# State space branch of a two-block model on one core: states of four pairs kept, output products issued by column group, input products on full-height tiles

## Chip, cores and metric

One Trainium2 chip, one core. The metric is the device time of one execution in microseconds (us). Three runs of the kernel before gave 3057.99, 3059.45 and 3059.55 us; the median is 3059.45 us.

## The reference

The kernel computes two blocks of a network on 256 tokens of width 2048 (272 tokens with 16 meta tokens in the first block). Block one projects the normed input into query and key-value latents, a signal u of width 1024 and two gates, runs latent attention and a diagonal state space model side by side, mixes both, and applies a feed-forward layer. Block two has an mLSTM layer and a banded attention layer. Only the state space model is touched by the change:

```
bu  = einsum(u, B_bar)                    # per group of 16 channels, 64 complex states
x_t = A_bar * x_{t-1} + bu_t              # 272 steps, complex
y   = Re(C x) + D u
y   = gelu(y);  ssm_out = (y @ w_val) * sigmoid(y @ w_gate)
```

There are 64 channel groups. Two of them make a *pair* (128 states, 32 channels), so there are 32 pairs, and they lie in eight blocks j of four pairs q.

## The kernel before, in words

**The main stream.** Nearly all work of TensorE is weight products in a two-part form. `split_chunk` (L397 to L406) loads a chunk of eight 128x128 weight blocks on SyncE's queue, ScalarE casts it to `hi` (L404), VectorE forms `lo = raw - hi` (L405); there are five `raw`, three `hi` and three `lo` buffers. `mm3` then issues for each block one product with `hi` over 512 columns (L430) and one with `lo` over 256 columns (L434); L432 and L433 take the place of L430 where 272 tokens are worked on. `Stream.take` counts a *tick* whenever a new chunk is begun, and each tick advances the side tasks that have been spawned.

**The side task.** `ssm` is a generator; `run` spawns it as `self.paced(self.ssm(), 2)`, so that one of its steps (from `yield` to `yield`) is written into the program every second tick, while the main stream works on the latents, the gates, attention (`mla`) and its projection (`attn_proj`). Before `ssm_out` and `mix` the task is finished. The order in which each engine then gets its instructions is set by a planner that simulates the program (`schedule_with_timeline_sim=True`); writes into one PSUM tile keep the order of the program.

**One turn of `ssm`** (g = 0 to 3) works on two blocks j = 2g and 2g+1, that is on eight pairs, and treats pair q of both blocks (index k = 0, 1) together:
- `ssm_matrices(j)` (L882 to L934): a 384 KB load issued from ScalarE's queue (L887) into the first 768 columns of `ssa[:, k, :]`, VectorE products of [128, 128] (L898 to L903, L919, L920 and others), four transposes (L909) into columns 768 to 1279, output matrices in columns 1280 to 1791, scratch `t1`, `t2` in columns 1792 to 2047, and the products for `k0` (L928). Those loop over q outside and the two parts i inside; each writes 32 partitions of PSUM, a column group of the array of its own for each q.
- 16 copies of u into `uu` (L958), in the form of [64 rows per pair]: two pairs share one tile, in its upper and lower half.
- for each q: four **input products** (L972), with a stationary tile of 64 rows and 128 columns over 136 columns; the rotation tables `cs`, `sn` (L975 to L980); a step later the rotated inputs (L982 to L987) and the scans (L992, L993); a step later the states `xr`, `xi` (L997 to L1002); a step later ten **output products** (L1009 to L1013), five for each k. Four of the five have 128 rows and 32 columns (L1009, L1010, L1012, L1013); the one with `k0` (L1011) has 32 rows and 32 columns. All ten of a pair write the same 32 partitions of the PSUM tile `yps`, which is taken at the head of the turn.
- at the end two additions into `yv` (L1017).

The states lie in `ws[2]` and `ws[4]`, which the tables of the next q overwrite (L976 writes `ws[2]`). Every fp32 product shows in the trace as two instructions ("x2"), each with its own weight load.

Of the kernel before, what the change touches and what calls it, by code (L numbers as in the profile page):

```python
# [8 lines left out]
F32 = mybir.dt.float32  # L9
# [3 lines left out]
ALU = mybir.AluOpType  # L13
AX = mybir.AxisListType

P = 128
D = 2048
KT = D // P
T = 256
NM = 16  # L20
TM = T + NM
# [279 lines left out]
class Builder:  # L301
# [50 lines left out]
    def sm(self, n=32):  # L352
        return self.t("s", [P, 32], bufs=20)[:, :n]
# [399 lines left out]
    def ssm_setup(self):  # L753
        nc = self.nc
        V = nc.vector
        w = self.pair(1, TM, dtype=F32).rearrange("p i k t -> p i (k t)")

        self.ssa, self.ssw = w[:, 0, :4096].rearrange("p (k n) -> p k n", k=2), w[:, 1, :]
        sm = self.sm
        ts = lambda o, x, s1, s2, op0, op1: V.tensor_scalar(o, x, s1, s2, op0, op1)  # L760
        tt = V.tensor_tensor
# [48 lines left out]
        step, x, mag = sm(), sm(), sm()  # L810
# [12 lines left out]
        nr, den, a, b = (sm() for _ in range(4))  # L823
# [17 lines left out]
        w = self.ssw  # L841
# [94 lines left out]
    def ssm(self):  # L936
        nc = self.nc
        yield from self.ssm_setup()
        tt = nc.vector.tensor_tensor
        mm = nc.tensor.matmul  # L940
        scan = nc.vector.tensor_tensor_scan
        NCH = TM // 2
        ws = [self.ssw[:, 1600 + i * TM : 1600 + (i + 1) * TM] for i in range(8)]
        cs, sn = ws[0], ws[1]

        uu = self.ssw[:, 1600 + 8 * TM : 1600 + 10 * TM].rearrange("p (k h c) -> p k h c", k=2, h=2)
        two = lambda ap: ap.rearrange("p (k c) -> p k c", k=2)
        m = lambda ap: ap.rearrange("p (k a b) -> p k a b", k=2, a=17)

        for g in range(4):  # L950
            k0 = []
            for j in (2 * g, 2 * g + 1):
                k0.append((yield from self.ssm_matrices(j)))
            for k in range(2):
                for q in range(4):
                    for e in range(2):
                        r = 64 * (q % 2) + 32 * e
                        nc.vector.tensor_copy(  # L958
                            uu[r : r + 32, k, q // 2, :], self.u[32 * q : 32 * q + 32, 2 * g + k, e, :]
                        )  # L960
            yield
            yps = self.aux()
            for q in range(4):
                rows = slice(32 * q, 32 * q + 32)
                p0 = slice(8 * g + q, 8 * g + q + 5, 4)
                pr, pi = self.aux(TM), self.aux(TM)
                r2 = slice(64 * (q % 2), 64 * (q % 2) + 64)
                for k in range(2):
                    c = slice(k * NCH, (k + 1) * NCH)
                    for ps, i in ((pr, 0), (pi, 1)):  # L970
                        o = 768 + 256 * i + P * (q // 2)
                        mm(ps[:, c], self.ssa[r2, k, o : o + P], uu[r2, k, q // 2, :], start=True, stop=True)  # L972
                a_ = [x[:, p0, :].unsqueeze(3).to_broadcast([P, 2, 17, 8]) for x in self.tabA]
                b_ = [x[:, p0, :].unsqueeze(2).to_broadcast([P, 2, 17, 8]) for x in self.tabB]
                tt(m(cs), a_[0], b_[0], ALU.mult)  # L975
                tt(m(ws[2]), a_[1], b_[1], ALU.mult)  # L976
                tt(cs, cs, ws[2], ALU.subtract)
                tt(m(sn), a_[1], b_[0], ALU.mult)
                tt(m(ws[3]), a_[0], b_[1], ALU.mult)
                tt(sn, sn, ws[3], ALU.add)  # L980
                yield
                tt(ws[2], pr, cs, ALU.mult)  # L982
                tt(ws[3], pi, sn, ALU.mult)
                tt(ws[2], ws[2], ws[3], ALU.add)
                tt(ws[4], pi, cs, ALU.mult)
                tt(ws[5], pr, sn, ALU.mult)
                tt(ws[4], ws[4], ws[5], ALU.subtract)  # L987
                for k in range(2):
                    c = slice(k * NCH, (k + 1) * NCH)
                    i = 8 * g + 4 * k + q  # L990
                    d = self.mag2[:, i : i + 1].to_broadcast([P, NCH])
                    scan(ws[3][:, c], d, ws[2][:, c], 0.0, ALU.mult, ALU.add)  # L992
                    scan(ws[5][:, c], d, ws[4][:, c], 0.0, ALU.mult, ALU.add)  # L993
                yield

                x = lambda ap: two(ap)[:, :, NM // 2 - 1 :]
                tt(x(ws[2]), x(ws[3]), x(cs), ALU.mult)  # L997
                tt(x(ws[6]), x(ws[5]), x(sn), ALU.mult)
                tt(x(ws[2]), x(ws[2]), x(ws[6]), ALU.subtract)
                tt(x(ws[4]), x(ws[5]), x(cs), ALU.mult)  # L1000
                tt(x(ws[7]), x(ws[3]), x(sn), ALU.mult)
                tt(x(ws[4]), x(ws[4]), x(ws[7]), ALU.add)  # L1002
                yield
                for k in range(2):
                    w = self.ssa[:, k, :]
                    o = k * NCH + NM // 2
                    xr, xi = ws[2][:, o - 1 :], ws[4][:, o - 1 :]
                    ev, od = yps[rows, k * T : k * T + P], yps[rows, k * T + P : (k + 1) * T]
                    mm(ev, w[:, 1536:1664][:, rows], xr[:, :P], start=True, stop=False)  # L1009
                    mm(ev, w[:, 1664:1792][:, rows], xi[:, :P], start=False, stop=False)  # L1010
                    mm(ev, k0[k][rows, :], self.u[rows, 2 * g + k, 0, NM // 2 :], start=False, stop=True)  # L1011
                    mm(od, w[:, 1280:1408][:, rows], xr[:, 1 : P + 1], start=True, stop=False)  # L1012
                    mm(od, w[:, 1408:1536][:, rows], xi[:, 1 : P + 1], start=False, stop=True)  # L1013
            eo = lambda ap: ap.rearrange("p (c e) -> p e c", e=2)
            for k in range(2):
                j = 2 * g + k
                nc.vector.scalar_tensor_tensor(  # L1017
                    eo(self.yv[:, j, :]), self.u[:, j, :, NM // 2 :], self.v("ssm_d", j),
                    two(yps[:, k * T : (k + 1) * T]), ALU.mult, ALU.add,
                )  # L1020
# [577 lines left out]
    def run(self):  # L1598
        self.setup()
        self.front()  # L1600
        self.ssm_in()
        ssm = self.spawn(self.paced(self.ssm(), 2))
        self.latents()
        self.conditioning(((150, 476), (510, 770)))
        self.gates()
        heads = self.mla()
        self.attn_proj(heads)
        self.finish(ssm)
        self.ssm_out()
        self.mix()  # L1610
        self.out_proj()
        self.ffn()
        self.enter2()
        self.probe("x1", self.x)
        state = self.layer0()
        while self.later:
            self.later.pop(0)[1]()
        self.layer1(*state)
# [33 lines left out]
```

## Time and profile before

| what | value |
|---|---|
| median of 3 runs | 3059.45 us |
| the profiled execution | 3057.36 us |
| span of its trace | 3055.6 us |
| busy: PE, VectorE, ScalarE, GpSimd | 98%, 76%, 48%, 2% |
| mean granted TensorE clock | 0.989 |
| chain that ended last | PE 97%, VectorE 2%, ScalarE 1% |
| the state space branch in the trace | about 47 to 600 us, from 128 us on with products |

The profiled execution is one run of its own. Its span is counted from the first to the last instruction; 1.8 us lie around it. A matmul's row gives its start and a modelled duration that overlaps the next one's, so the cost of a product is read from the distance between starts.

### The profile page before, as it was taken

The numbers are of one execution on the slowest core, as the hardware profiler recorded it, in microseconds if no ns is written. First come the engines' busy times: TensorE is split into PE (matmuls) and PEld (weight loads), VectorE is DVE, ScalarE is ACT, GpSimd is POOL, SyncE is SP. The second block draws the span as 40 slices with busy tenths as digits, with TensorE's granted clock in tenths as the row PEclk, the third lists the DMA queues.
The fourth block names the chain that finished last, engine by engine and source line by source line (L and its number), as shares of the span: only waits on it lengthen the run. The fifth ranks groups of instructions, "written<-read, shape, count | busy, mean of one in ns | idle before, by whom it ended". The sixth has DMA issues, their size and how long they took to land.

```text
span 3055.6 us, 46404 instructions
## 1 busy us (share of the span) xinstructions
PE 2998.4 (98%) x17170; PEld 2573.7 (84%) x17170; DVE 2327.8 (76%) x4641; ACT 1479.0 (48%) x2360; POOL 75.4 (2%) x139
## 2 busy tenths in 40 slices
PE   8899999999999999999999999999999999999987
PEld 8878888788888888888888888888888888888876
DVE  7988855689888778878878878877777778546555
ACT  5433355455544444434455444444444555445554
POOL 0000000000000000000000000000000001000000
PEclk9999999999999999999999999999999999999998
DMA  7545522498878888878756677778777765665544
GB/s 243 164 144 174 173 83 83 146 318 273 275 274 277 270 279 270 278 267 268 262 182 200 227 259 249 249 261 268 257 256 250 236 188 183 188 193 179 178 158 129
DMA packets 187139, 673.06 MB, mean 220 GB/s; under 512 B 21280, under 2 KB 23456, under 8 KB 186656
## 3 DMA queue, kind: packets, MB, share of 16 engines
q1 hardware_dynamic: 179568, 649.12, 65.3%
q0 software_dynamic: 4128, 15.73, 1.5%
q10 hardware_dynamic: 3216, 5.24, 0.5%
q8 instruction: 134, 2.20, 0.3%
q14 instruction: 93, 0.76, 0.1%
HBM read 661.63 MB, written 8.39 MB: 219 GB/s over the span
## 4 chain that ended last, share of the span: by engine, by line
PE 97%; DVE 2%; ACT 1%; issue 0%; POOL 0%; DMA 0%; SPq 0%; ACTq 0%; DVEq 0%; POOLq 0%
PE acc L430 50%; PE acc L434 26%; PE acc L479 3%; PE acc L478 3%; PE acc L477 3%; PE acc L432 1%; PE acc L433 1%; PE aux L972 1%; PE aux L1071 1%; PE aux L1383 0%; DVE lo L405 0%; PE aux L1070 0%; PE aux L1540 0%; PE aux L1361 0%; PE aux L1012 0%; PE aux L1011 0%
## 5 line engine op out<-in xcount | busy, mean ns | idle before, releaser
L430 PE MATMUL acc<-big,hi 128*128 128x512 f32 x6592 | 2323.6, 397 | 8.3 <-DVE big L1220 3.0
L434 PE MATMUL acc<-big,lo 128*128 128x256 f32 (+1 forms) x6832 | 1912.9, 282 | 2.2 <-DVE lo L405 2.0
L404 ACT ACTIVATE hi<-raw 128x1024 fp32r<-128x1024 f32 (+1 forms) x969 | 1025.5, 1059 | 1304.4 <-PE acc L430 807.1
L405 DVE TENSOR_TENSOR lo<-raw,hi 128x1024 fp32r<-128x1024 f32 (+1 forms) x969 | 1183.1, 1221 | 558.2 <-ACT hi L404 550.9
L430 PEld LDWEIGHTS acc<-big,hi 128*128 128x128 f32 x6592 | 1237.8, 188 | 297.7 <-issue 5.3
L434 PEld LDWEIGHTS acc<-big,lo 128*128 128x128 f32 x6832 | 1288.8, 189 | 14.6 <-DVE lo L405 4.2
L626 DVE SCALAR_TENSOR_TENSOR raw<-raw,gemv 128x512 f32<-128x512 f32 x512 | 332.2, 685 | 0.0
L477 PE MATMUL acc<-hi,big 128*128 128x512 f32 (+1 forms) x480 | 178.0, 371 | 0.3 <-DVE qr L442 0.3
L478 PE MATMUL acc<-hi,big 128*128 128x512 f32 (+1 forms) x480 | 177.3, 369 | 0.0
L479 PE MATMUL acc<-lo,big 128*128 128x512 f32 (+1 forms) x480 | 169.2, 375 | 0.0
L442 DVE TENSOR_TENSOR t<-t,acc 128x256 f32<-128x256 f32 x276 | 114.0, 414 | 6.7 <-ACT t L441 6.6
L441 ACT ACTIVATE t<-acc 128x256 f32<-128x256 f32 x276 | 100.9, 367 | 14.0 <-PE acc L434 12.1
L477 PEld LDWEIGHTS acc<-hi,big 128*128 128x128 f32 x480 | 90.1, 188 | 16.0 <-DVE qr L442 0.6
L478 PEld LDWEIGHTS acc<-hi,big 128*128 128x128 f32 x480 | 90.2, 188 | 15.3 <-issue 0.3
L479 PEld LDWEIGHTS acc<-lo,big 128*128 128x128 f32 x480 | 89.4, 188 | 15.5 <-issue 1.0
L432 PE MATMUL acc<-big,hi 128*128 128x272 f32 x240 | 70.2, 295 | 7.9 <-ACT hi L404 7.9
L447 DVE TENSOR_TENSOR big<-big,acc 128x256 f32<-128x256 f32 x160 | 65.3, 415 | 13.2 <-PE acc L434 12.4
L433 PE MATMUL acc<-big,hi 128*128 128x272 f32 x240 | 69.9, 293 | 0.0
L489 DVE TENSOR_TENSOR ss<-ss,t 128x256 f32<-128x256 f32 (+1 forms) x132 | 54.5, 422 | 2.5 <-ACT t L488 2.1
L432 PEld LDWEIGHTS acc<-big,hi 128*128 128x128 f32 x240 | 46.0, 192 | 8.8 <-ACT hi L404 7.9
L1323 DVE SCALAR_TENSOR_TENSOR t<-qr,vec,t 128x256 f32<-128x256 f32 x96 | 46.1, 480 | 1.0
L433 PEld LDWEIGHTS acc<-big,hi 128*128 128x128 f32 x240 | 46.1, 192 | 0.0
(360 smaller groups left out, 1953.2 us busy)
## 6 DMA issues: line engine op xcount, KB each, us to landing
raw<-in_w_l_dram SPq DMA_DIRECT2D x482, 512.0 KB, 4.2
raw<-in_w_ffn_dram SPq DMA_DIRECT2D x264, 512.0 KB, 4.4
raw<-in_w_ada_dram SPq DMA_DIRECT2D x256, 512.0 KB, 4.5
raw<-in_w_in_dram SPq DMA_DIRECT2D x97, 512.0 KB, 3.7
raw<-in_w_mix_dram SPq DMA_DIRECT2D x64, 512.0 KB, 4.4
raw<-in_w_out_dram SPq DMA_DIRECT2D x32, 512.0 KB, 4.5
raw<-in_w_up_dram SPq DMA_DIRECT2D x28, 512.0 KB, 3.5
gates_d<-qa POOLq DMA_DIRECT2D x16, 256.0 KB, 2.9
```

Of the source, the lines that this page charges most:

```text
L404: nc.scalar.activation(hi[:, c], raw[:, c], AF.Copy)
L405: self.last_lo = nc.vector.tensor_tensor(lo[:, c], raw[:, c], hi[:, c].bitcast(F32), ALU.subtract)
L430: mm(both, wh, x[:, :, kt, :], start=(kt == 0), stop=False)
L432: mm(ps[:, :n], wh, x[:, 0, kt, :], start=(kt == 0), stop=False)
L433: mm(ps[:, :n], wh, x[:, 1, kt, :], start=False, stop=False)
L434: mm(ps[:, :n], wl, x[:, 0, kt, :], start=False, stop=last)
L441: self.nc.scalar.activation(dst, ps[:, n : 2 * n], AF.Copy)
L442: self.nc.vector.tensor_tensor(dst, dst, ps[:, :n], ALU.add)
L477: mm(ps, xh[:, kt, b:e], wh, start=(kt == 0), stop=False)
L478: mm(ps, xl[:, kt, b:e], wh, start=False, stop=False)
L479: mm(ps, xh[:, kt, b:e], wl, start=False, stop=(kt == nk - 1))
L626: nc.vector.scalar_tensor_tensor(raw[:, j, :], raw[:, j, :], 0.5, st["c"], ALU.mult, ALU.mult, accum_out=st["sum"][:, 2 * i + j : 2 * i + ...
```

## The change

The states of all four pairs of a turn get buffers of their own (`xs`): five of the eight in the columns 0 to 644 of `ssa`, which hold the loaded matrices until they have been used, one in the scratch columns from 1792 on, two in `ssw`. The ten output products of the four pairs leave the loop over q and come after one more `yield`, the loop over q innermost, so that four products in a row write the four column groups. `yps` is taken only then. `uu` has a tile of 128 rows for each q and k, zero outside the pair's 64 rows, zeroed once on GpSimd; the input products take all 128 rows. The copies take both k at once: 8 in place of 16 for a turn. `ws` has five buffers in place of eight. A further `yield` stands ahead of the additions into `yv`.

```diff
-        w = self.pair(1, TM, dtype=F32).rearrange("p i k t -> p i (k t)")
-        self.ssa, self.ssw = w[:, 0, :4096].rearrange("p (k n) -> p k n", k=2), w[:, 1, :]
+        w = self.pair(1, TM, dtype=F32).rearrange("p i k t -> p (i k t)")
+        self.ssa, self.ssw = w[:, :4096].rearrange("p (k n) -> p k n", k=2), w[:, 4096:]
...
+        uu = self.ssw[:, o : o + 8 * NCH].rearrange("p (k q c) -> p k q c", k=2, q=4)
+        nc.gpsimd.memset(uu, 0.0)
+        xs = [self.ssa[:, :, i * NX : (i + 1) * NX] for i in range(5)] + [self.ssa[:, :, 1792 : 1792 + NX]]
...
-                        mm(ps[:, c], self.ssa[r2, k, o : o + P], uu[r2, k, q // 2, :], start=True, stop=True)
+                        mm(ps[:, c], self.ssa[:, k, o : o + P], uu[:, k, q, :], start=True, stop=True)
...
-                for k in range(2):
-                    w = self.ssa[:, k, :]
...
-                    mm(ev, w[:, 1536:1664][:, rows], xr[:, :P], start=True, stop=False)
-                    mm(ev, w[:, 1664:1792][:, rows], xi[:, :P], start=False, stop=False)
-                    mm(ev, k0[k][rows, :], self.u[rows, 2 * g + k, 0, NM // 2 :], start=False, stop=True)
-                    mm(od, w[:, 1280:1408][:, rows], xr[:, 1 : P + 1], start=True, stop=False)
-                    mm(od, w[:, 1408:1536][:, rows], xi[:, 1 : P + 1], start=False, stop=True)
+
+            yps = self.aux()
+            for k in range(2):
+                w = self.ssa[:, k, :]
+                for o, n, i, c0 in ((0, 1536, 0, 0), (0, 1664, 1, 0), (0, None, 0, 0), (P, 1280, 0, 1), (P, 1408, 1, 1)):
+                    for q in range(4):
+                        rows = slice(32 * q, 32 * q + 32)
+                        out = yps[rows, k * T + o : k * T + o + P]
+                        if n is None:
+                            mm(out, k0[k][rows, :], self.u[rows, 2 * g + k, 0, NM // 2 :], start=False, stop=True)
+                        else:
+                            mm(
+                                out, w[:, n : n + P][:, rows], xs[2 * q + i][:, k, c0 : c0 + P],
+                                start=(i == 0), stop=(c0 == 1 and i == 1),
+                            )
+            yield
```

## Rows read from the trace of the kernel before

**Rows 1.** The page: shares of the chain that ended last.
```profile
PE 97%; DVE 2%; ACT 1%; issue 0%; POOL 0%; DMA 0%; SPq 0%; ACTq 0%; DVEq 0%; POOLq 0%
```

**Rows 2.** Busy time by stretch: length, PE, PEld, DVE, ACT, POOL, clock, DMA share, GB/s.
```profile
160.00:380.00 220.00, 220.00 (x1341) 178.85 (x1339) 190.44 (x451) 77.36 (x106) 10.37 (x15) 1.00 0.54 167
380.00:600.00 220.00, 219.49 (x1373) 174.32 (x1373) 133.18 (x317) 109.97 (x259) 6.13 (x13) 1.00 0.33 102
```

**Rows 3.** Timeline of PE, one pair's output products: start, duration, instruction, count.
```profile
206.29 0.40 PE L430 MATMUL acc<-big,hi 128*128 128x512 f32 x1
206.52 0.28 PE L434 MATMUL acc<-big,lo 128*128 128x256 f32 x1
206.65 0.39 PE L430 MATMUL acc<-big,hi 128*128 128x512 f32 x1
...
212.93 0.39 PE L430 MATMUL acc<-big,hi 128*128 128x512 f32 x1
213.25 0.41 PE L1009 MATMUL aux<-big 128*32 128x128 f32 x2
213.59 0.39 PE L434 MATMUL acc<-big,lo 128*128 128x256 f32 x1
...
214.25 0.41 PE L1010 MATMUL aux<-big 128*32 128x128 f32 x2
...
215.16 0.38 PE L1013 MATMUL aux<-big 128*32 128x128 f32 x2
215.38 0.38 PE L1009 MATMUL aux<-big 128*32 128x128 f32 x2
...
216.80 0.50 PE L430 MATMUL acc<-big,hi 128*128 128x512 f32 x1
217.13 0.28 PE L434 MATMUL acc<-big,lo 128*128 128x256 f32 x1
```

**Rows 4.** Timeline of PE: the small products L928, alone and in a burst.
```profile
220.85 0.25 PE L928 MATMUL aux<-big 128*32 128x32 f32 x2
221.03 0.66 PE L909 MATMUL aux<-cst,big 128*128 128x128 f32 x4
...
227.91 0.48 PE L928 MATMUL aux<-big 128*32 128x32 f32 x28
228.33 0.39 PE L434 MATMUL acc<-big,lo 128*128 128x256 f32 x1
```

**Rows 5.** Timeline of PE: input products, and full-height fp32 products (L909).
```profile
162.79 0.28 PE L434 MATMUL acc<-big,lo 128*128 128x256 f32 x1
163.00 0.73 PE L972 MATMUL aux<-big 64*128 64x136 f32 x4
163.66 0.50 PE L430 MATMUL acc<-big,hi 128*128 128x512 f32 x1
...
187.80 0.38 PE L909 MATMUL aux<-cst,big 128*128 128x128 f32 x2
187.93 0.36 PE L434 MATMUL acc<-big,lo 128*128 128x256 f32 x1
188.13 0.40 PE L430 MATMUL acc<-big,hi 128*128 128x512 f32 x1
```

**Rows 6.** Line L972: count, min/median/max ns, first and last start.
```profile
L972 PE MATMUL aux<-big x128: 276/276/592, 128.7 to 562.7; 64*128 64x136 f32 x128
```

**Rows 7.** Waits of DVE, 128 to 620 us: total, times, longest.
```profile
DVE big L976 <- PE aux L1012: 17.5, 8, 3.2
```

**Rows 8.** DMA issues, one line: count, KB each, us to landing.
```profile
big<-in_ssm_dram ACTq DMA_DIRECT2D x8, 384.0 KB, 4.4
```

**Rows 9.** Lines L900, L1017, L1131: count, min/median/max ns, first and last start.
```profile
L900 DVE TENSOR_TENSOR big<-big x16: 277/284/293, 76.6 to 439.4; 128x128 f32<-128x128 f32 x16
L1017 DVE SCALAR_TENSOR_TENSOR big<-big,vec,aux x8: 473/479/483, 216.9 to 598.7; 128x256 f32<-128x256 f32 x8
L1131 DVE SCALAR_TENSOR_TENSOR big<-t,t x16: 399/418/426, 568.8 to 648.3; 128x256 f32<-128x256 f32 x16
```

More of the change, by code (lines that the diff above doesn't have):

```diff
@@ L942, in ssm @@
         NCH = TM // 2
-        ws = [self.ssw[:, 1600 + i * TM : 1600 + (i + 1) * TM] for i in range(8)]
-        cs, sn = ws[0], ws[1]
-        uu = self.ssw[:, 1600 + 8 * TM : 1600 + 10 * TM].rearrange("p (k h c) -> p k h c", k=2, h=2)
+        NX = T // 2 + 1
+        ws = [self.ssw[:, 1600 + i * TM : 1600 + (i + 1) * TM] for i in range(5)]
+        cs, sn, t1, t2, t3 = ws
+        o = 1600 + 5 * TM
+        uu = self.ssw[:, o : o + 8 * NCH].rearrange("p (k q c) -> p k q c", k=2, q=4)
+        nc.gpsimd.memset(uu, 0.0)
+        xs = [self.ssa[:, :, i * NX : (i + 1) * NX] for i in range(5)] + [self.ssa[:, :, 1792 : 1792 + NX]]
+        rest = self.ssw[:, o + 8 * NCH : o + 8 * NCH + 4 * NX].rearrange("p (k i c) -> p k i c", k=2, i=2)
+        xs += [rest[:, :, 0, :], rest[:, :, 1, :]]
         two = lambda ap: ap.rearrange("p (k c) -> p k c", k=2)
@@ L953, in ssm @@
                 k0.append((yield from self.ssm_matrices(j)))
-            for k in range(2):
[L955 to L960, printed above, removed]
+            for q in range(4):
+                for e in range(2):
+                    r = 64 * (q % 2) + 32 * e
+                    nc.vector.tensor_copy(
+                        uu[r : r + 32, :, q, :], self.u[32 * q : 32 * q + 32, 2 * g : 2 * g + 2, e, :]
+                    )
             yield
-            yps = self.aux()
             for q in range(4):
-                rows = slice(32 * q, 32 * q + 32)
                 p0 = slice(8 * g + q, 8 * g + q + 5, 4)
                 pr, pi = self.aux(TM), self.aux(TM)
-                r2 = slice(64 * (q % 2), 64 * (q % 2) + 64)
                 for k in range(2):
@@ L975, in ssm @@
                 tt(m(cs), a_[0], b_[0], ALU.mult)
-                tt(m(ws[2]), a_[1], b_[1], ALU.mult)
-                tt(cs, cs, ws[2], ALU.subtract)
+                tt(m(t1), a_[1], b_[1], ALU.mult)
+                tt(cs, cs, t1, ALU.subtract)
                 tt(m(sn), a_[1], b_[0], ALU.mult)
-                tt(m(ws[3]), a_[0], b_[1], ALU.mult)
-                tt(sn, sn, ws[3], ALU.add)
+                tt(m(t2), a_[0], b_[1], ALU.mult)
+                tt(sn, sn, t2, ALU.add)
                 yield
-                tt(ws[2], pr, cs, ALU.mult)
@@ L983, in ssm @@
[L983 to L993, printed above, removed]
+                tt(t1, pr, cs, ALU.mult)
@@ new lines, in ssm @@
+                tt(t2, pi, sn, ALU.mult)
+                tt(t1, t1, t2, ALU.add)
+                tt(t2, pi, cs, ALU.mult)
+                tt(t3, pr, sn, ALU.mult)
+                tt(t2, t2, t3, ALU.subtract)
+                for a, b in ((t1, t3), (t2, t1)):
+                    for k in range(2):
+                        c = slice(k * NCH, (k + 1) * NCH)
+                        i = 8 * g + 4 * k + q
+                        scan(b[:, c], self.mag2[:, i : i + 1].to_broadcast([P, NCH]), a[:, c], 0.0, ALU.mult, ALU.add)
@@ L994, in ssm @@
                 yield
                 x = lambda ap: two(ap)[:, :, NM // 2 - 1 :]
[L997 to L1002, printed above, removed]
-                yield
-                for k in range(2):
-                    w = self.ssa[:, k, :]
-                    o = k * NCH + NM // 2
-                    xr, xi = ws[2][:, o - 1 :], ws[4][:, o - 1 :]
-                    ev, od = yps[rows, k * T : k * T + P], yps[rows, k * T + P : (k + 1) * T]
-                    mm(ev, w[:, 1536:1664][:, rows], xr[:, :P], start=True, stop=False)
-                    mm(ev, w[:, 1664:1792][:, rows], xi[:, :P], start=False, stop=False)
-                    mm(ev, k0[k][rows, :], self.u[rows, 2 * g + k, 0, NM // 2 :], start=False, stop=True)
-                    mm(od, w[:, 1280:1408][:, rows], xr[:, 1 : P + 1], start=True, stop=False)
-                    mm(od, w[:, 1408:1536][:, rows], xi[:, 1 : P + 1], start=False, stop=True)
@@ new lines, in ssm @@
+                xr, xi = xs[2 * q], xs[2 * q + 1]
+                tt(xr, x(t3), x(cs), ALU.mult)
+                tt(x(t2), x(t1), x(sn), ALU.mult)
+                tt(xr, xr, x(t2), ALU.subtract)
+                tt(xi, x(t1), x(cs), ALU.mult)
+                tt(x(t2), x(t3), x(sn), ALU.mult)
+                tt(xi, xi, x(t2), ALU.add)
+                yield
+            yps = self.aux()
+            for k in range(2):
+                w = self.ssa[:, k, :]
+                for o, n, i, c0 in ((0, 1536, 0, 0), (0, 1664, 1, 0), (0, None, 0, 0), (P, 1280, 0, 1), (P, 1408, 1, 1)):
+                    for q in range(4):
+                        rows = slice(32 * q, 32 * q + 32)
[6 more added lines that the diff above has]
+                                start=(i == 0), stop=(c0 == 1 and i == 1),
+                            )
```

## The prediction

> **What bounds the kernel now.** I read the chain that ended last first: PE holds 97% of it [rows 1], so an instruction taken off PE counts in full unless another engine takes over. The branch runs beside the main stream from 128 to 600 us, so next come the busy times of that part. PE is busy all the time in both halves; VectorE is busy 190.4 of 220 us in the first and 133.2 in the second [rows 2]. PE is thus the bound, with VectorE close behind in the first half. Busy PE is not PE at its peak, so the prices below are distances between starts on PE's timeline.
>
> The main stream alternates L430 and L434, 0.23 us from the one to the other and 0.13 us back [rows 3]. An excursion to the output products breaks this. The pair shown takes 0.34 us (213.25 to 213.59) and 2.55 us (214.25 to 216.80). Going in costs 0.09 us more than the normal step (212.93 to 213.25, 0.32 for 0.23), or 0.08 us from an L434 (0.21 for 0.13 [rows 5]). The first step of the main stream afterwards is 0.10 us too long (216.80 to 217.13) [rows 3]. That makes 0.34 + 2.55 + 0.09 + 0.08 + 2 x 0.10 = 3.26 us for a pair, and 16 pairs make 52.2 us.
>
> Streaming is only part of this: two instructions of 128 columns with no change of shape between them take 0.22 us (215.16 to 215.38), 0.11 each [rows 3]. The 18 of the longer visit make 1.98 us. The other 0.57 us are five changes of tile shape, 0.11 us each: into and out of the 32-row product twice, and back to the full tile.
>
> **Output products after.** A turn still has 40 of them, 80 instructions, and there are four turns. What changes is that neighbours write different column groups. The trace has such neighbours once: L928. Two instructions of it alone hold PE for 0.18 us, 28 in a burst for 0.42 us [rows 4], so 26 more cost 0.24 us, 9 ns each. At 0.11 us for 128 columns one of 32 columns would take 27 ns alone. Column groups therefore overlap threefold in this burst. Start-up should count for less in products four times as long, so I take 3.5, between this and the four that are there: 80 x 0.11 / 3.5 = 2.5 us. The shapes change four times in a turn (two visits to the `k0` products) for 0.44 us, and one excursion costs 0.30 us (in 0.09, out 0.11, next step 0.10). All 40 write one PSUM tile and keep their order, and the last pair's `xr` and `xi` come after the other pairs', as the lone L1009 at 213.25 shows for `xr` [rows 3]. So I expect two short excursions ahead, 0.30 us each. A turn is then 3.85 us and the four 15.4 us: **36.8 us less**. Bounds: with fourfold overlap and no early excursions 2.9 us for a turn, 40 us less; with no overlap 80 x 0.11 + 1.34 = 10.1 us, 12 us less.
>
> A rule speaks for less. The burst itself runs against any strict order: its code issues four passes in a row to one column group before it goes to the next, and if each pass waited for the one ahead of it to start, only the last of one group and the first of the next would overlap, so 28 would take about 21 x 27 ns = 0.57 us, where 0.42 with the way out was measured [rows 4]. The Trainium skill, in "TensorE: Matmul & The Clock Gate", Part 3 (The mechanism), says that matmuls start and end in strict program order. The trace does not agree with it here; by that rule the turn would take 5.7 us and the gain be 29 us.
>
> **Input products after.** A visit of four instructions costs 0.08 us going in, 0.66 us itself and 0.10 us afterwards [rows 5], 0.84 us. On 128 rows nothing changes shape: 136 columns at the rate above are 0.117 us, four 0.47 us, and after the full-height fp32 products L909 the next step is 0.20 instead of 0.13 us [rows 5], so 0.54 us. That is 0.30 us less a visit. The 128 instructions [rows 6] are 32 fours; some share a visit, so I take 0.25 for each: **8 us less**. Bounds: 0 (the way in costs the same for any fp32 product) and 10.
>
> **VectorE.** The wait of L976 for the output products, 17.5 us in all [rows 7], goes, because the tables no longer overwrite states that a product reads. It is not PE's time, so it is worth nothing by itself; it is the room that VectorE needs. The 16 copies become 8 of twice the length, about nothing. Three scratch buffers in place of six force an order on dependent operations; some tenths of a us for a pair, hidden as long as PE is last. But PE's work in the first half shrinks by some 9 of 16 pairs, 25 us: VectorE's 190 us stand against 195 [rows 2]. The lower cast L405 of the main stream is on that engine too. I charge 3 us for it, with bounds of 0 and 10.
>
> **Moved work and queues.** The loads of the next turn's matrices must now wait until this turn's last output product has read `xs`, which lies where they land. They are issued on ScalarE's queue, and behind them stand the casts L404. A load takes 4.4 us [rows 8]. ScalarE's issue waits only if it comes ahead of the product; a further step (two ticks) lies between, and the casts are up to three `hi` buffers ahead, two chunks of 8 x 0.36 us = 5.8 us. I take 0, with a bound of 3 x 4.4 = 13 us. The clearing of `uu` on GpSimd is hidden behind the set-up. Four more steps make eight ticks, 23 us later for the end of the branch: the last L1017 starts at 598.7 us, and the attention projection ends with L1131 at 648.3 us [rows 9], so 50 us of room shrink to 27. Nothing waits for that. `yps` is held for less time, which can only help.
>
> **The sum.** 36.8 + 8 - 3 = 41.8 us. The profiled execution of 3057.36 us would become 3015.6; it lies 2.1 us below the median, so for the median 3059.45 - 41.8 = **3018 us**.
>
> **Rivals.**
> - *Passes start in program order.* Each fp32 product is two passes on one column group, so only neighbours overlap: 4.4 us of streaming for a turn in place of 2.5, 7.6 us less gain, 3025 us. For it: every product is issued as two instructions; against it: the burst [rows 4]. The rule of the Trainium skill quoted above says this. Chance 0.09.
> - *The planner splits a turn.* The products of three pairs are ready first; taken at once, they overlap threefold (60 x 0.11 / 3 = 2.2 us), and the last pair's 20 run alone (2.2 us), with a second set of shape changes (0.44): 2.6 us more a turn, 3028 us. Against it: today L1009 goes ahead alone, and the products that need only `xr` too stay behind it [rows 3]. Chance 0.07.
> - *VectorE becomes the bound of the first half.* Then this half gains no more than the 17.5 us of waits that vanish [rows 7] in place of 25: 3026 us. Chance 0.08.
> - *No overlap at 128 columns:* 25 us less gain, 3043 us. The burst shows only 32 columns. Chance 0.04.
> - *Slower: a turn's start is exposed.* At three boundaries the load can no longer run ahead. If PE sits through load and matrix products of both blocks, 2 x (4.4 [rows 8] + 19 operations x 0.28 us [rows 9]) = 19 us, three boundaries cost 58 us: 3076 us. It decides from 14 us a boundary on (41.8 / 3). For it: the loads were always early, so the trace shows no such wait. Against it: the main stream is there to fill the time, and the branch ended 50 us early. Chance 0.10, of which 0.04 for a draw.
>
> **How the numbers follow.** My forecast has what is left, 0.62. All cases but the last are faster by well over 0.2% (6 us, about what a measurement of this kernel can tell from no change): faster 0.90, same 0.04, slower 0.06. The range goes down to 3005 us (both gains at their upper bound, 40 + 10, no charge for VectorE, and a few us from a new order) and up to 3036, which takes in the first three rivals and the load's bound; it leaves out the last two.
>
> **What would show it.** Right: output lines in four bursts of about 3 to 4 us, starts within tens of ns in rows of the four column groups; L972 in the 128x128 form with the next main-stream step near its normal distance; no wait of L976 for PE; PE still at 97% of the chain. Wrong: starts of the burst 0.11 us apart, two separate bursts for a turn, waits of L434 for L405 between 160 and 380 us, or PE idle at the first L909 of a turn.

## The result and the profile after

The changed kernel takes **3008.69 us** (median of 4 runs, 3003.41 to 3013.44), the kernel before beside it 3059.5 us (4 runs, 3057.99 to 3059.65). The ratio is 0.9834, 95% interval 0.9822 to 0.9846: 50.8 us less, where 41.8 were forecast. The profiled execution took 3007.21 us with a span of 3005.4 us; against the profiled execution of before the span is 50.2 us shorter, and the rows below account for that difference.

The chain that ended last, from the page of the changed kernel. It still belongs to PE, as in [rows 1]:

```profile
PE 97%; DVE 2%; ACT 1%; DMA 0%; issue 0%; POOL 0%; SPq 0%; ACTq 0%; DVEq 0%; POOLq 0%
```

Busy times by stretch, changed kernel (columns as in [rows 2]; the branch now ends near 567 us, so the last stretch ends at 560):

```profile
128.00:160.00 32.00, 28.19 (x159) 24.43 (x158) 30.18 (x71) 12.91 (x22) 2.57 (x3) 0.95 0.44 141
160.00:380.00 220.00, 220.00 (x1487) 187.68 (x1486) 200.15 (x467) 94.95 (x157) 10.18 (x14) 1.00 0.56 178
380.00:560.00 180.00, 180.00 (x1191) 147.21 (x1190) 125.40 (x299) 92.61 (x213) 7.24 (x15) 1.00 0.40 122
```

From 160 us on PE is busy all the time, as before; it gets 1487 matmuls into the 220 us that held 1341 [rows 2]. VectorE has risen to 200 of 220 us and still does not hold PE up. The first row is new: this stretch was not among the rows of the prediction. The same stretch before:

```profile
128.00:160.00 32.00, 23.92 (x132) 18.39 (x130) 27.92 (x78) 9.98 (x22) 4.58 (x3) 0.73 0.35 112
```

PE was idle for 8 of 32 us there and its mean granted clock was 0.73; now it idles for 4 at 0.95.

**The output products** of one turn, timeline of PE (columns as in [rows 3]):

```profile
422.99 0.28 PE L434 MATMUL acc<-big,lo 128*128 128x256 f32 x1
423.20 0.65 PE L1017 MATMUL aux<-big 128*32 128x128 f32 x16
423.77 0.42 PE L1015 MATMUL aux<-big,k 32*32 32x128 f32 x8
424.12 1.09 PE L1017 MATMUL aux<-big 128*32 128x128 f32 x32
425.15 0.42 PE L1015 MATMUL aux<-big,k 32*32 32x128 f32 x8
425.50 0.65 PE L1017 MATMUL aux<-big 128*32 128x128 f32 x16
426.07 0.51 PE L1078 MATMUL aux<-ka,qa 128*128 128x144 f32 x2
```

All 80 instructions of a turn take 2.87 us (423.20 to 426.07); before, one pair's last 18 took 2.55 [rows 3]. The 32 of the middle row hold PE for 1.03 us (424.12 to 425.15), that is 32 ns each, or eight rounds of 0.13 us with the change of shape in it. Before, one pass alone took 0.11. But only this turn goes in one burst. In the three others 14 of the 80 instructions go ahead in short visits, ten visits in all, such as this one:

```profile
207.53 0.39 PE L430 MATMUL acc<-big,hi 128*128 128x512 f32 x1
207.85 0.43 PE L1017 MATMUL aux<-big 128*32 128x128 f32 x8
208.20 0.39 PE L434 MATMUL acc<-big,lo 128*128 128x256 f32 x1
208.43 0.39 PE L430 MATMUL acc<-big,hi 128*128 128x512 f32 x1
```

It costs 0.35 us itself, 0.09 going in (0.32 in place of 0.23) and 0.11 behind it (0.23 in place of 0.12). Over all visits I add up the distance from the first start of a visit to the next instruction of the main stream, and what the steps before and behind it exceed their normal length. For the changed kernel that is 14.2 + 1.3 + 1.4 = 16.9 us in 14 visits, for the kernel before 47.9 + 2.4 + 2.2 = 52.5 us in 26. The output products gave **35.6 us**.

**The input products**, timeline of PE:

```profile
162.81 0.28 PE L434 MATMUL acc<-big,lo 128*128 128x256 f32 x1
162.92 0.63 PE L974 MATMUL aux<-big 128*128 128x136 f32 x4
163.30 0.48 PE L430 MATMUL acc<-big,hi 128*128 128x512 f32 x1
163.62 0.28 PE L434 MATMUL acc<-big,lo 128*128 128x256 f32 x1
```

Four take 0.38 us in place of 0.66 [rows 5], the way in is the normal 0.11, and the step behind is 0.32 for 0.23. Added up in the same way they fall from 24.7 to 15.8 us: **8.9 us**. (Behind one of the visits, at 143.70 us, the next start comes 3.15 us too late because PE waits for L442; that is left out of the 15.8 and counted below, where the idle part of it is 2.9.)

35.6 + 8.9 = 44.5 us. Nearly all of the other 5.7 of the 50.2 us lies in the stretch from 128 to 160 us. Waits of PE there, before:

```profile
PE aux L519 <- POOL s L511: 5.6, 1, 5.6
PE aux L503 <- DVE ss L489: 2.5, 1, 2.5
```

and after:

```profile
PE acc L430 <- DVE t L442: 2.9, 1, 2.9
PE aux L519 <- POOL s L511: 0.9, 1, 0.9
```

8.1 us of idle time against 3.8. Behind the longer idle times the granted clock was at the lower of its two levels (1.2 GHz) from 142.3 to 159.3 us, behind the shorter ones from 147.1 to 150.5. Busy times of these two stretches (columns as in [rows 2]), first the kernel before, then the changed one:

```profile
142.30:159.30 17.00, 11.39 (x44) 7.76 (x44) 13.63 (x41) 3.02 (x9) 4.04 (x2) 0.50 0.24 71
147.10:150.50 3.40, 3.30 (x10) 2.81 (x11) 3.40 (x11) 0.00 (x0) 0.00 (x0) 0.50 0.02 5
```

Work at half clock costs half of its time, and only while PE is busy: the wait of 5.6 us lies inside the first of these stretches and is counted already. So the stretch from 128 to 160 us lost 8.1 + 11.4 / 2 = 13.8 us before and 3.8 + 3.3 / 2 = 5.5 us after, 8.3 us less. Of these, 3.2 us are output and input products that ran at half clock (20 passes of output products took 5.1 us in place of 2.9, eight of input products 2.1 in place of 1.1); they are in the prices already. That leaves 5.1 of the 5.7 us.

After the branch the two kernels roughly keep their distance: the difference between the starts of the same main-stream product (L430 and L432 counted) is 47.2 us at the 1300th (630 us of the changed kernel, behind the branch), 47.3 at the 5000th and 49.4 at the 6800th (2948 us).

Waits of VectorE between 128 and 620 us, changed kernel: two that the change made. The wait of L976 for output products [rows 7] is gone.

```profile
DVE big L898 <- DMA big<-in_ssm_dram: 5.6, 3, 2.6
DVE big L984 <- PE aux L974: 1.6, 3, 0.7
```

### The profile page after: what moved, and what is told of

Read it like the earlier page. It is cut to its first block, busy times and chain, and to the rows that moved or that the text cites. A ratio compares the mean times of both kernels' runs of the same rounds, so it can differ in the third digit from the quotient of the medians.

```text
span 3005.4 us, 46365 instructions
## 1 busy us (share of the span) xinstructions
PE 2953.7 (98%) x17170; PEld 2551.4 (85%) x17170; DVE 2322.7 (77%) x4609; ACT 1478.4 (49%) x2360; POOL 74.2 (2%) x140
## 4 chain that ended last, share of the span: by engine, by line
PE 97%; DVE 2%; ACT 1%; DMA 0%; issue 0%; POOL 0%; SPq 0%; ACTq 0%; DVEq 0%; POOLq 0%
PE acc L430 50%; PE acc L434 27%; PE acc L479 3%; PE acc L477 3%; PE acc L478 3%; PE acc L432 1%; PE acc L433 1%; PE aux L1079 1%; DVE lo L405 0%; PE aux L1391 0%; PE aux L974 0%; PE aux L1078 0%; PE aux L1548 0%; PE aux L1017 0%; PE aux L1369 0%; ACT hi L404 0%
## 5 line engine op out<-in xcount | busy, mean ns | idle before, releaser
L430 PE MATMUL acc<-big,hi 128*128 128x512 f32 x6592 | 2321.8, 397 | 10.9 <-DVE big L1228 3.1
L434 PE MATMUL acc<-big,lo 128*128 128x256 f32 (+1 forms) x6832 | 1913.3, 282 | 2.0 <-DVE lo L405 1.7
L405 DVE TENSOR_TENSOR lo<-raw,hi 128x1024 fp32r<-128x1024 f32 (+1 forms) x969 | 1183.7, 1222 | 551.6 <-ACT hi L404 544.1
L430 PEld LDWEIGHTS acc<-big,hi 128*128 128x128 f32 x6592 | 1239.4, 188 | 297.4 <-issue 3.6
L434 PEld LDWEIGHTS acc<-big,lo 128*128 128x128 f32 x6832 | 1289.8, 189 | 12.6 <-DVE lo L405 4.9
L442 DVE TENSOR_TENSOR t<-t,acc 128x256 f32<-128x256 f32 x276 | 114.2, 414 | 8.1 <-ACT t L441 7.9
L432 PE MATMUL acc<-big,hi 128*128 128x272 f32 x240 | 70.6, 296 | 7.9 <-ACT hi L404 7.9
L432 PEld LDWEIGHTS acc<-big,hi 128*128 128x128 f32 x240 | 46.3, 193 | 8.3 <-ACT hi L404 7.9
```

Source lines behind the costliest of these rows:

```text
L405: self.last_lo = nc.vector.tensor_tensor(lo[:, c], raw[:, c], hi[:, c].bitcast(F32), ALU.subtract)
L430: mm(both, wh, x[:, :, kt, :], start=(kt == 0), stop=False)
L432: mm(ps[:, :n], wh, x[:, 0, kt, :], start=(kt == 0), stop=False)
L434: mm(ps[:, :n], wl, x[:, 0, kt, :], start=False, stop=last)
L442: self.nc.vector.tensor_tensor(dst, dst, ps[:, :n], ALU.add)
```

## The experiments

Twelve kernels ran on three chips, each with the kernel before beside it: 3059.47 us (8 runs) for the first four, 3059.22 (15 runs) for the next four, 3061.05 (9 runs) for the last four. Prices of output and input products are added up as above.

**1. The output part alone.** The changed kernel with the input products on 64 rows again:

```diff
-        uu = self.ssw[:, o : o + 8 * NCH].rearrange("p (k q c) -> p k q c", k=2, q=4)
-        nc.gpsimd.memset(uu, 0.0)
+        uu = self.ssw[:, o : o + 4 * NCH].rearrange("p (k h c) -> p k h c", k=2, h=2)
...
-                        mm(ps[:, c], self.ssa[:, k, o : o + P], uu[:, k, q, :], start=True, stop=True)
+                        mm(ps[:, c], self.ssa[r2, k, o : o + P], uu[r2, k, q // 2, :], start=True, stop=True)
```

> The output part alone: the changed kernel with the input products put back on tiles of 64 rows. Theory (the terms of the sum add: excursions priced from PE's starts, output products 52.5 us before and 16.9 after, input products 24.7 before and about 15.8 after): the output gain of 35.6 us stays, the input gain of about 9 goes, so 3059.5 - 36 - (0 to 6 for the stall near 140 us) = 3017 to 3024 us, with L972's successor again 0.84 us a visit. Rival (the input products' tile shape costs nothing, since PE would wait in any case): like the changed kernel, 3003 to 3013 us.

Measured: 3018.23 us (3012.61 to 3020.07), ratio 0.9864 (0.985 to 0.9879); output products 16.9 us, input products 25.3. It gains 41.2 us, 5.6 more than the price of the output products fell. PE waits 0.9 + 0.6 us between 128 and 160 us.

**2. The input part alone.** The kernel before with zero-padded full-height input tiles and the merged copies:

```diff
...
+        uu = self.ssw[:, 1600 + 7 * TM : 1600 + 11 * TM].rearrange("p (k q c) -> p k q c", k=2, q=4)
+        nc.gpsimd.memset(uu, 0.0)
...
-                        mm(ps[:, c], self.ssa[r2, k, o : o + P], uu[r2, k, q // 2, :], start=True, stop=True)
+                        mm(ps[:, c], self.ssa[:, k, o : o + P], uu[:, k, q, :], start=True, stop=True)
```

> The input part alone: the kernel before with zero-padded full-height input products and the merged copies, output products untouched (seven scratch buffers in place of eight). Theory: 9 us less than before from the tile shape, 3050 us, or down to 3044 if the stall near 140 us shrinks as well. Rival (worth nothing): 3059 us, within 0.2% of before.

Measured: 3049.85 us (3044.61 to 3052.56), ratio 0.9967 (0.9954 to 0.998); input products 16.9 us, output products 53.8. It gains 9.6 us, and the two parts add up: 41.2 + 9.6 = 50.8, the gain of the whole change. PE waits 3.9 + 2.1 us in the stretch from 128 to 160, less than before (5.6 + 2.5) but far from the 0.9 + 0.6 of run 1. Its gain is 3 us more than its prices explain (7.8 less for input products, 1.3 more for output products), so a part of what was not foreseen comes with the input part too; the larger part, 5.6 us, comes with the output part. Run 1 holds all of the output part: the place of the products, the new buffers and the new order of the scans. These were not separated.

**3. The ten products of a pair in a row**, at the new place in the program:

```diff
-            for k in range(2):
...
+            order = [(k, q, p) for q in range(4) for k in range(2) for p in prods]
+            for k, q, (o, n, i, c0) in order:
...
```

> The changed kernel with the 40 output products of a turn in the same place, but all ten of a pair in a row (the loop over q outermost). Theory (neighbouring column groups overlap, and that is the gain): streaming goes back to one at a time, 80 x 0.109 = 8.7 us for a turn, and the shape changes go from 4 to 16, 1.3 us more: 10.2 to 10.5 us in place of 2.9 us for the burst, 30 us in all, 3036 to 3042 us. Rival (what counts is that there are four long excursions in place of 32 short ones, not the order inside): 3005 to 3015 us. Between them, if PE looks far ahead across pairs: 3015 to 3030 us.

Measured: 3035.54 us (3034.68 to 3036.33), ratio 0.9923 (0.9906 to 0.994), half a us under the range that was expected; output products 43.6 us. One pair on PE's timeline in this kernel:

```profile
216.01 0.40 PE L430 MATMUL acc<-big,hi 128*128 128x512 f32 x1
216.33 0.41 PE L1017 MATMUL aux<-big 128*32 128x128 f32 x2
216.67 0.40 PE L1015 MATMUL aux<-big,k 32*32 32x128 f32 x2
217.00 1.07 PE L1017 MATMUL aux<-big 128*32 128x128 f32 x8
218.00 0.40 PE L1015 MATMUL aux<-big,k 32*32 32x128 f32 x2
218.33 0.62 PE L1017 MATMUL aux<-big 128*32 128x128 f32 x4
218.88 0.50 PE L430 MATMUL acc<-big,hi 128*128 128x512 f32 x1
```

This is the plainest picture of the change. Here 8 instructions on one column group take 1.00 us (217.00 to 218.00). In the changed kernel 32 on four column groups take 1.03 (424.12 to 425.15). The same products, at the same place in the program, cost 26.7 us less when the four groups are neighbours (43.6 - 16.9), and the time is 26.9 us less (3035.54 - 3008.69).

**4. Two products of one pair in a row**, that is four passes on one column group before the next group's four:

```diff
-            for k in range(2):
...
+            order = [(k, q, p) for k in range(2) for s in (prods[0:2], prods[2:3], prods[3:5]) for q in range(4) for p in s]
+            for k, q, (o, n, i, c0) in order:
...
```

> The changed kernel with the output products of a turn ordered so that two products of a pair, four passes on one column group, come in a row before the next pair's (same number of shape changes as the changed kernel). Theory A (PE starts a later column group's pass while an earlier group's queue waits, as the small products L928 showed): no difference, 3003 to 3014 us, starts of four groups interleaved. Theory B (passes start in program order): of 16 passes only the last and first of neighbours overlap, 13 steps of 0.109 us in place of 4, 1 us more in each of four segments of a turn, 16 us in all, 3019 to 3029 us.

Measured: 3010.41 us (3008.99 to 3011.41), ratio 0.9841 (0.9827 to 0.9856): no difference from the changed kernel. In PE's timeline the 32 instructions of the middle group take 1.05 us (423.15 to 424.20):

```profile
423.15 1.12 PE L1017 MATMUL aux<-big 128*32 128x128 f32 x32
424.20 0.42 PE L1015 MATMUL aux<-big,k 32*32 32x128 f32 x8
```

If each pass waited for the start of the one ahead of it in the program, 16 passes would have only three overlaps, the 32 about 26 x 0.11 = 2.9 us. In the trace they come in eight rounds of four, some 0.11 us from round to round, and the four starts of a round are 8 to 37 ns apart. The four groups fill up beside each other whichever comes first in the program. (That the instructions do come in the program's order rests on all 40 products writing one PSUM tile; runs 10 and 11, where no product goes ahead of the one put first, bear that out.) Its price of 19.6 us, 2.7 more than the changed kernel's, comes from 17 visits in place of 14.

**5. A step boundary ahead of the products and none behind them**, to get rid of the ten short visits. (In the changed kernel only the boundary that ends the loop over q, which was there before, lies between the last pair's states and the products.)

```diff
+            yield
             yps = self.aux()
...
-            yield
             eo = lambda ap: ap.rearrange("p (c e) -> p e c", e=2)
```

> The changed kernel with the step boundary behind the output products moved ahead of them: four ticks instead of two lie between the last pair's states and the products, none between the products and the next turn's load. Theory (the ten short visits ahead of the bursts cost 0.34 to 0.36 us and 0.2 us around each, because the last pair's states come late): each turn is one burst as the third one is, 3.1 us in place of 4.4 to 5.0, 4.6 us in all: 3002 to 3006 us against 3008.7. Rival (the load, now right behind the products on ScalarE's queue, holds up the casts): up to 13 us lost, 3009 to 3022 us, with a wait of the cast or of PE at the turns.

Measured: 3008.23 us (3006.18 to 3009.56), ratio 0.9833 (0.982 to 0.9847), and still 14 visits with 17.0 us. A miss: the step in which a product is written does not hold it back, as the same 14 visits show; the planner seems to place a product as soon as its states are there. (Run 9 gets rid of the visits in another way.)

**6. As run 5, with the `k0` products of both halves as neighbours**, two changes of tile shape in a burst in place of four:

```diff
...
+            order = (
+                od + [(0, 1536, 0, 0, True, False), (0, 1664, 1, 0, False, False), (0, None, 0, 0, False, True)],
+                [(0, None, 0, 0, True, False), (0, 1536, 0, 0, False, False), (0, 1664, 1, 0, False, True)] + od,
+            )
...
```

> As the run with the boundary moved ahead, and the order inside a turn changed so that the k0 products of both halves are neighbours: two shape changes in place of four. Theory (a shape change costs PE about 0.1 us): 0.2 us less for each burst, below 2.7 us for 80 instructions with the way out, 1 us in all: 3001 to 3005 us. Rival (changes are hidden behind the overlap): bursts as long as before.

Measured: 3009.36 us (3005.36 to 3011.02), ratio 0.9832 (0.9819 to 0.9846). The products themselves take 13.45 us in place of 14.2, about what eight changes of shape at 0.11 us are worth; the time does not show it, so the forecast of 3001 to 3005 us was a miss, and PE has a new wait of 1.3 us for L442.

**7. The changed kernel with an empty first step**, which puts the branch two ticks later against the main stream, and **8. the kernel before with the same step**:

```diff
     def ssm(self):
+        yield
```

> The changed kernel with one empty step ahead of the branch, so that all of it is written two ticks later. Theory (PE's idle time and the half clock between 137 and 160 us depend on how the branch's VectorE work falls among the steps of the second latent norm, which the planner decides): idle and half clock there change by several us one way or the other, the products cost the same (17 us output, 16 to 19 us input): 3002 to 3020 us. Rival (the shorter idle time belongs to the change itself): 4 us of idle and 3 to 10 us at half clock as in the changed kernel, 3004 to 3013 us.

> The kernel before with the same empty step ahead of the branch. Theory (order decides): the 8 us of idle time and 17 us of half clock near 140 us shrink or grow by several us, the rest stays: 3050 to 3066 us with the products at 52 and 25 us. Rival (the idle time belongs to the output products' place in the old order): 3057 to 3062 us with 8 us of idle time.

Measured: run 7 3017.26 us (3011.93 to 3017.62), ratio 0.9859 (0.9846 to 0.9873); run 8 3056.35 us (3052.93 to 3061.83), ratio 0.9991 (0.9982 to 1.0). Between 128 and 160 us the phase does little: run 7 has a clock of 0.95 there, like the changed kernel, run 8 has 0.73, like the kernel before. The 8.6 us that run 7 loses lie at the other end of the branch. PE there, waits from 128 to 620 us and then the timeline:

```profile
PE acc L430 <- DVE big L412: 6.0, 1, 6.0
```

```profile
592.55 0.28 PE L434 MATMUL acc<-big,lo 128*128 128x256 f32 x1
598.87 0.77 PE L430 MATMUL acc<-big,hi 128*128 128x512 f32 x1 [6.03 <-DVE big L412]
599.43 0.41 PE L434 MATMUL acc<-big,lo 128*128 128x256 f32 x1
```

The value projection of the branch needs gelu(y) split in two parts (L412), and gelu waits for the last addition L1026 (L1025 in the changed kernel). Timelines of ScalarE and of VectorE in that stretch of run 7:

```profile
592.45 1.91 ACT L1035 ACTIVATE big<-big 128x2048 f32<-128x2048 f32 x1 [2.65 <-DVE big L1026]
...
595.48 2.18 ACT L411 ACTIVATE big<-big 128x512 fp32r<-128x512 f32 x4
```

```profile
598.04 1.89 DVE L412 TENSOR_TENSOR big<-big,big 128x512 fp32r<-128x512 f32 x3
```

From the end of the branch (592.4 us) to the first split there are some 6 us of other engines' work, and the clock falls behind the wait: it is 0.50 from 598.8 to 604.3 us, and L430 to L434 takes 0.42 us in place of 0.23. In the changed kernel the gelu starts at 566.64 us, and the product that waits here (the same one in the count of L430) starts at 594.27 us, without a wait.

So the gelu of run 7 comes 25.8 us later, although two ticks are only some 6 us (2 x 8 x 0.36). The last pair's operations on VectorE end at 585.9 us in run 7 (L1005) and at 558.1 us in the changed kernel (L1004), and in run 7 they lie far apart, among operations of the main stream. What spread them was not tested. The time of run 7 lies in the range of its theory, but not by that theory: the stretch near 140 us changed little.

**9. to 11. No product can go ahead.** The first product of a turn is made one that needs the last pair's states. Writes into `yps` keep their order, so nothing behind it can be early. Run 9 runs the inner loop from pair 3 down; run 10 also takes the product with `xi` ahead of the one with `xr`; run 11 also makes the `k0` products neighbours, as in run 6. Run 12 is the changed kernel itself on the same chip.

```diff
-                for o, n, i, c0 in ((0, 1536, 0, 0), (0, 1664, 1, 0), (0, None, 0, 0), (P, 1280, 0, 1), (P, 1408, 1, 1)):
-                    for q in range(4):
+                for o, n, i, c0 in ((0, 1664, 1, 0), (0, 1536, 0, 0), (0, None, 2, 0), (P, 1408, 1, 1), (P, 1280, 0, 1)):
+                    for q in (3, 2, 1, 0):
...
-                                start=(i == 0), stop=(c0 == 1 and i == 1),
+                                start=(i == 1), stop=(c0 == 1 and i == 0),
```

(This is run 10; run 9 has the line with `(3, 2, 1, 0)` alone.)

> The changed kernel with the innermost loop of the output products run from pair 3 down to pair 0. Theory (writes into one PSUM tile keep the program's order, and the ten short visits of the changed kernel are the products of pairs whose states are ready early): the first product now needs the last pair's xr, so at most one short visit for a turn is left, of products that need xr only; 4 to 8 excursions in place of 14, and 2 to 4 us less than the changed kernel beside it. Rival (the planner places ready work by its own estimate and gives back elsewhere what it saves, as with the two kernels that moved the step): fewer excursions, but the time within 1.5 us of the changed kernel. Second rival: the order of writes isn't kept, still 14 excursions, same time.

> As the run with the last pair first, and in each group of products the one with xi ahead of the one with xr. Theory: xi of the last pair is the last state of a turn, so nothing can go ahead: exactly 4 excursions of 80 instructions, each about 2.95 us and 3.1 with the way in and out, 12.4 us in all in place of 16.9, so 4 to 5 us less than the changed kernel beside it. Rival: the whole burst lies later and delays the next turn's load and matrices, and what is saved on PE comes back as waits; within 1.5 us of the changed kernel or slower.

> As the run with the last state first, and the k0 products of both halves k made neighbours, so that the tile shape changes twice in a burst and not four times. Theory: two changes of 0.11 us less in each of four bursts, 0.9 us less than the run with the last state first, 5 to 6 us less than the changed kernel. Rival: as there, the gain on PE comes back as waits.

> The changed kernel itself, on the same chip as the three others: 3003 to 3014 us, median near 3008.

| run | median, us | range | ratio to before | visits | output products, us |
|---|---|---|---|---|---|
| 12, changed kernel | 3009.67 | 3006.17 to 3012.42 | 0.9832 (0.9819 to 0.9846) | 14 | 16.9 |
| 9, last pair first | 3003.04 | 3000.45 to 3005.86 | 0.9811 (0.9798 to 0.9825) | 7 | 13.0 |
| 10, last state first | 3006.16 | 3002.62 to 3009.02 | 0.9821 (0.9807 to 0.9834) | 4 | 12.0 |
| 11, and `k0` joined | 3005.23 | 3002.83 to 3006.99 | 0.9818 (0.9805 to 0.9832) | 4 | 11.0 |

A burst of run 10, and one of run 11 (its L1022 and L1020 are the L1017 and L1015 of the others), timeline of PE:

```profile
209.98 0.64 PE L1017 MATMUL aux<-big 128*32 128x128 f32 x16
210.55 0.42 PE L1015 MATMUL aux<-big,k 32*32 32x128 f32 x8
210.90 1.08 PE L1017 MATMUL aux<-big 128*32 128x128 f32 x32
211.91 0.42 PE L1015 MATMUL aux<-big,k 32*32 32x128 f32 x8
212.26 0.65 PE L1017 MATMUL aux<-big 128*32 128x128 f32 x16
212.84 0.39 PE L434 MATMUL acc<-big,lo 128*128 128x256 f32 x1
```

```profile
209.86 1.08 PE L1022 MATMUL aux<-big 128*32 128x128 f32 x32
210.87 0.64 PE L1020 MATMUL aux<-big,k 32*32 32x128 f32 x16
211.44 1.08 PE L1022 MATMUL aux<-big 128*32 128x128 f32 x32
212.45 0.39 PE L434 MATMUL acc<-big,lo 128*128 128x256 f32 x1
```

2.86 us for a turn's 80 instructions with four changes of shape, 2.59 with two. Visits and prices come out as expected, and all four runs of run 9 are below all four of run 12. Runs 10 and 11 are faster than run 12 by 3.5 and 4.4 us in their medians, about the 4.9 and 5.9 us of their prices, but their ranges overlap with its range. Runs 9 to 11 can't be told apart by time; the 1.0 us by which run 11 is cheaper on PE than run 10 is smaller than the spread of either.

The 6.6 us of run 9 are more than its price explains (3.9), and the traces do not show the rest in the branch. At the 1300th product, just behind it, run 9 is 4.4 us ahead of the first trace of the changed kernel and 1.6 us ahead of run 12's. Run 12 loses another 7.5 us against run 9 after that, where the kernels do the same work. The two traces of the changed kernel differ in the same way: run 12 is 2.8 us ahead at that product and 5.2 us behind at the end. So differences of a few us between single executions say nothing of the branch.

## Why the prediction was right

**Output products: 36.8 forecast, 35.6 measured.** The mechanism is the one given, and run 3 shows it by taking only the overlap away. Two sizes were off, and that they nearly cancel is luck. Overlap is almost fourfold at 128 columns, where 3.5 was taken: the 2.87 us of the one-burst turn stand beside 80 x 0.11 / 4 = 2.2 for streaming, 0.44 for four changes of shape and 0.11 for the way out, 2.75 in all. Against that the three other turns have ten short visits where eight in four turns were expected, at some 0.5 us each and not 0.30. The 0.30 holds the way in, the way out and the next step; the working left out that a visit of two or four passes holds PE nearly as long as one of eight (0.34 us; the one shown has 0.35), so its streaming is hardly overlapped. Run 10 gives the size: four bursts alone cost 12.0 us, the changed kernel 16.9.

**Input products: 8 forecast, 8.9 measured**, in the step named: the way in is free, and a visit itself is 0.28 us shorter, where 0.66 - 0.47 = 0.19 was worked out.

**VectorE: 3 charged, 0 measured.** It is busy 200 of 220 us and PE 220 of 220; L434 waits for L405 once, for 0.4 us. Near to full is not full: its own waits shrank with the work taken off PE.

**The rivals.** *Passes in program order* falls with run 4. The rule of the Trainium skill that the prediction weighed ("TensorE: Matmul & The Clock Gate", Part 3, The mechanism: matmuls start and end in program order) does not hold for the neighbouring column groups of these traces; by it run 4 would have lost about 1.9 us in each group of 32. *A turn that is split* happened in a small form, the ten short visits: 4.9 us (16.9 - 12.0) where 10 were worked out. *No overlap* falls with run 3, which is what it would look like (3035.5; 3043 was worked out). *An exposed start of a turn* was half right: the load is late, and VectorE waits 5.6 us for it in three turns, but PE has the main stream to do and loses nothing. Run 5 makes these waits longer (7.2 us) and is no slower.

**What the prediction missed** makes most of the difference between 41.8 and 50.8. It read the stretch from 160 us on and not the 32 us ahead of it. A row of the windows for 128 to 160 us would have shown a clock of 0.73 and 8 us of idle PE, time that a shift of the branch can win or lose. Runs 1, 2 and 8 show that most of this part comes with the output part of the change: every kernel with the products in the old place has 6 us of idle time or more there and a clock of 0.73 to 0.79, every one with the new place under 4.5 us and 0.84 to 0.95. Whether the place of the products, the new buffers or the new order of the scans does it was not tested, and which instruction decides it is only argued: GpSimd's L511, on which PE's L519 waits. The range of the prediction allowed "a few us from a new order"; the sum had no term for it.

**A step without a price, measured at the wrong place.** "50 us of room shrink to 27. Nothing waits for that" held in the changed kernel: its branch ends 37 us ahead of the last L1139 of the attention projection (566.1 and 603.3 us), and PE does not wait for it. But the attention projection is not all that the end of the branch can run into. The gelu and its split stand in the program behind the branch, and the product that needs the first split is due at 594.3 us. Run 7, one step longer at its head, ran into that and paid 6.0 us of wait and half-clock time behind it.

## What to carry to other kernels

fp32 products with 32 output columns are cheapest when the four column groups stand close together in the program, in turn or two products of a group at a time (run 4): 32 passes then take the time of 8, and the states that this needs kept are worth their buffers. When a group of products is meant to go in one burst, let its first product be the one that needs the last operand; a step boundary does not hold the others back. Before a side task is moved or lengthened, read the stretches at both of its ends for idle time and for the granted clock, not only the stretch in which the work itself shrinks.

## What the hardware showed that was not expected

- Column groups overlap fully even if the program issues four passes of one group before the next (run 4: 1.05 us for 32 passes, 1.03 in alternation).
- The same GpSimd operation L511 (3 elements on each partition) took 3.12 us in the kernel before and 0.92 after:

```profile
145.01 3.12 POOL L511 TENSOR_TENSOR s<-s,mhalf 128x3 f32<-128x3 f32 x1 [20.43 <-DVE s L536]
```

```profile
140.28 0.92 POOL L511 TENSOR_TENSOR s<-s,mhalf 128x3 f32<-128x3 f32 x1 [18.42 <-DVE s L536]
```

  In the first case VectorE ran eight operations with two inputs one behind the other beside it (L979 at 144.86 to L980 at 146.99), in the second a scan, which has two inputs too, and then two such operations. Run 2 had 2.27 us, run 8 4.13, all other runs 0.92. The Trainium skill says in "SBUF — State Buffer", Who interferes with whom, that a VectorE operation with two inputs in SBUF and a GpSimd operation that reads SBUF shut each other out, the second until the first is done. That agrees in direction; but L511 lost some 2.2 us, more than the 0.42 of any one of those operations. In each of the three slow cases it ended 0.71 to 0.72 us behind the VectorE operation after which VectorE first paused (L980 at 147.42 us in the kernel before, L1001 at 145.24 in run 2, with a pause of 0.035 us, L899 at 145.03 in run 8), as if it had to let the whole unbroken row pass. A row of two-input operations is not enough to explain it, though: an earlier L511 of the kernel before (2 elements, at 123.74 us) took 0.84 us beside L975, L976 and L978, which follow each other without a pause. No run here moved L511 by itself, so the cause stays open.
